# High weights against both halves of the activations in one 512-column product: the up-projections of a two-layer encoder

## The chip, the core and the metric

The kernel runs on one core of a Trainium2 chip. The metric is the device time of one execution in microseconds (us); of several runs the median is taken. PE is TensorE, PEld its weight load, DVE is VectorE, ACT is ScalarE, POOL is GpSimd, SP is SyncE, which issues the DMAs.

## What is computed

The reference is a trunk of two layers on 256 tokens of width 2048: a token mixer (attention), then a channel mixer, each with a normalization before and after and with shifts, scales and gates that come from a conditioning vector. The channel mixer is the part that the change touches, with `D_FF` = 5504:

```python
def conv_ffn(h, w_up, conv_w, conv_b, w_down):
    gate, up = jnp.split(h @ w_up, 2, axis=-1)
    gp = jnp.pad(gate, ((0, 0), (1, 1), (0, 0)))
    gate = gp[:, :-2] * conv_w[0] + gp[:, 1:-1] * conv_w[1] + gp[:, 2:] * conv_w[2] + conv_b
    return (jax.nn.gelu(gate, approximate=True) * up) @ w_down
```

All of it is in float32. The convolution runs over the tokens, with three taps per feature.

## The kernel before

**Products in three parts.** A float32 product is made of products of rounded halves: each operand is a high part (its rounding to the type `fp32r`) plus a low part (the rest). Of the four products of halves three are computed: high weights with high activations, high weights with low activations, low weights with high activations. The activations of the up-projection stand in the tile `hT`, laid out `[128, 16, 2, 256]`: 16 tiles of 128 input features (k), then high and low, then 256 tokens. So the high and low halves of one k-tile lie side by side, 512 columns in a row.

**The stream of weights.** All weights pass through one stream (class `Stream`, object `st`), in an order that a plan fixes. A unit of 512 KB (128 x 1024) lands in one of nine `raw` buffers. ScalarE copies it to its high part `whi` (line 259), VectorE subtracts to get the low part `wlo` (line 309, method `lows`). There are four buffers of each (`SPLIT_BUFS`), so a unit can be split once PE has finished the unit four before it. Between the weight units lie units of the modulation matrix `ada_w`, which VectorE multiplies and adds up itself (line 284).

**Ticks.** When PE's products of a unit have been written down, `st.done` is called: it frees the unit's buffers, lets the stream go on (which writes down the split of a further unit and any modulation steps), makes one tick of a clock of units, and then writes down the low parts. `st.chain` spreads the steps that follow an accumulator over the ticks after it, one step per tick, so that they stand between the splits on ScalarE and VectorE.

**The channel mixer** (`ffn`, line 1031) works on two parts of the 5504 features, 22 and 21 blocks of 128. In each part it takes two blocks at a time: 256 features of the gate, then the same 256 of the up side. One accumulator is one PSUM bank, seen as two blocks of 256 tokens (`packed`). `feat_units` (line 639) runs over the 16 k-tiles, four to a unit, and for each block makes three products of 256 columns, with the weights as the stationary operand: lines 655, 657 and 658. There are eight banks, handed out in turn.

After the gate's accumulator `gate` lets ScalarE write the middle tap with the bias to `cv`, at once; one tick later VectorE adds the two outer taps, reading the bank; one tick later ScalarE applies the gelu. After the up accumulator, `up` lets VectorE multiply `cv` with the bank (line 1058), one tick later ScalarE rounds it to the high half of `act`, and one tick later VectorE subtracts for the low half. When a part is done, `out_chunks` multiplies `act` with the down-projection's weights in products of 512 columns (lines 622 to 624).

In layer 0 the first seven accumulators (`PRE`) are built side by side before the rest, over k-tiles as they become ready. In layer 1 the first accumulator is begun while the normalization before it is still running (`f_head`), and finished in the loop.

Of the kernel before, what the change touches and what calls it, by code (L numbers as in the profile page):

```python
# [9 lines left out]
F32 = mybir.dt.float32  # L10
F32R = mybir.dt.float32r
I32 = mybir.dt.int32
AF = mybir.ActivationFunctionType
# [3 lines left out]
D, S, P = 2048, 256, 128  # L17
KT = D // P
DFF = 5504
NF = DFF // P  # L20
# [168 lines left out]
def encoder_kernel(ctx: ExitStack, tc: tile.TileContext, x, c, ada_w, ada_b, norm_g,  # L189
                   ab_w_in, ab_w_out, a_sink, c_w_in, c_w_out, c_lambda, c_subln_g,  # L190
                   ffn_w_up, ffn_conv_w, ffn_conv_b, ffn_w_down, out):
    nc = tc.nc
# [6 lines left out]
    def bank():  # L199
        return psum.tile([P, 512], F32, name="bank", bufs=8)  # L200
# [4 lines left out]
    def vy():  # L205
        return cp.tile([P, 2, D], F32, name="vy")
# [187 lines left out]
    st = Stream()  # L394
    mods, cur = {}, {}
# [81 lines left out]
    def sums():  # L477
        s = small("ssq", 5)
        nc.gpsimd.memset(s[:, 4:5], EPS)
        return s  # L480
# [8 lines left out]
    def square_sum(src, dst, n=D):  # L489
        j = tmp.tile([P, 512], F32, name="junk", bufs=1)  # L490
        nc.scalar.activation(j[:, :src.shape[1]], src, AF.Square, scale=n ** -0.5, accum_out=dst)  # L491
# [147 lines left out]
    def feat_units(acc, k0, kn, n):  # L639

        hT = cur["hT"]
        kt = k0
        while kt < k0 + kn:
            i, (hi, lo) = st.take()
            a = hi.shape[1]
            for b in range(a):
                k = kt + b
                for j in range(n // P):
                    wh = hi[:, b, j * P:(j + 1) * P]
                    if lo is None:  # L650
                        nc.tensor.matmul(acc[:, j], wh, cur["h"][:, k], start=k == 0 and j == 0, stop=k == KT - 1,
                                         skip_group_check=True)
                        continue
                    wl = lo[:, b, j * P:(j + 1) * P]
                    nc.tensor.matmul(acc[:, j], wh, hT[:, k, 0], start=k == 0 and j == 0, stop=False,  # L655
                                     skip_group_check=True)
                    nc.tensor.matmul(acc[:, j], wh, hT[:, k, 1], start=False, stop=False, skip_group_check=True)  # L657
                    nc.tensor.matmul(acc[:, j], wl, hT[:, k, 0], start=False, stop=k == KT - 1,  # L658
                                     skip_group_check=True)
            kt += a  # L660
            st.done(i)

    def packed():
        return bank().rearrange("p (j n) -> p j n", j=2)

# [6 lines left out]
    def feat_pair(pool, scale, name, bufs=1):  # L672
        acc = packed()
        feat_units(acc, 0, KT, 256)
        return feat_out(pool, acc, scale, name, bufs)
# [355 lines left out]
    def ffn(l, pool, next_norm, pre=0, head=None, first=()):  # L1031
        y = None
        ssq = [sums() for t in range(2)]
        cw = cwc[l]

        def gate(acc, cv, j, nj):
            def taps(_):
                for i in range(nj):
                    w0, w2 = cw[:, j + i:j + i + 1], cw[:, 2 * NF + j + i:2 * NF + j + i + 1]
                    nc.vector.scalar_tensor_tensor(cv[:, i, 1:], g[:, i, :S - 1], w0, cv[:, i, 1:],  # L1040
                                                   op0=ALU.mult, op1=ALU.add)
                    nc.vector.scalar_tensor_tensor(cv[:, i, :S - 1], g[:, i, 1:S], w2, cv[:, i, :S - 1],
                                                   op0=ALU.mult, op1=ALU.add)

            def gelu(_):
                nc.scalar.activation(cv[:, :nj], cv[:, :nj], AF.Gelu_apprx_tanh)

            g = acc
            for i in range(nj):
                w = cw[:, NF + j + i:NF + j + i + 1]  # L1050
                nc.scalar.activation(cv[:, i], g[:, i, :S], AF.Identity,
                                     bias=cw[:, 3 * NF + j + i:3 * NF + j + i + 1], scale=w)
            st.chain(taps, gelu)

        def up(acc, cv, act, j, nj):
            c = cv[:, :nj]
            ah = act[:, j:j + nj, 0]
            st.chain(lambda _: nc.vector.tensor_mul(c, acc[:, :nj], c),
                     lambda _: nc.scalar.activation(ah, c, AF.Copy),
                     lambda _: nc.vector.tensor_tensor(act[:, j:j + nj, 1], c, ah.bitcast(F32), op=ALU.subtract))  # L1060

        for part, (f0, fn) in enumerate(PARTS):
            act = pool.tile([P, 22, 2, S], F32R, name="act", bufs=1)
            p = pre if part == 0 else 0
            accs = [packed() for _ in range(p)]
            for n, (k0, k1) in enumerate(zip(FK, FK[1:])) if p else ():
                if n:
                    st.advance(plan.mid[n - 1])
                    st.flush()
                for k in range(k0, k1, 4):  # L1070
                    for t in range(2):
                        Affine(t, k, cur[t][:, k:k + 4], mods[0, 4], mods[0, 3], AFF1[t]).high().low()
                st.advance()
                for a in range(p):
                    feat_units(accs[a], k0, k1 - k0, 2 * P)
                    if k1 == KT:
                        if a % 2 == 0:
                            cv = pool.tile([P, 2, S], F32, name="cv", bufs=2)
                            gate(accs[a], cv, a, 2)
                        else:  # L1080
                            up(accs[a], cv, act, a - 1, 2)
            with tc.manual_schedule(engines=ORDERED) if pre else nullcontext():
                for j in range(p // 2 * 2, fn, 2):
                    nj = min(2, fn - j)
                    for k in range(2):
                        if j + k < p:
                            continue
                        if first:
                            acc = first.pop()
                            feat_units(acc, 4, KT - 4, nj * P)  # L1090
                        else:
                            acc = packed()
                            feat_units(acc, 0, KT, nj * P)
                        if k == 0:
                            cv = pool.tile([P, 2, S], F32, name="cv", bufs=2)
                            gate(acc, cv, f0 + j, nj)
                        else:
                            up(acc, cv, act, j, nj)
                final = part == len(PARTS) - 1
                y = y or vy()  # L1100

                def evac(acc, t, ch, then=None):
                    c0 = ch * 512
                    yc = y[:, t, c0:c0 + 512]
                    if part == 0:
                        nc.scalar.activation(yc, acc, AF.Copy)
                        return
                    z = tmp.tile([P, 512], F32, name="hf", bufs=3) if final else yc
                    nc.vector.tensor_add(z, acc, yc)
                    if final:  # L1110
                        square_sum(z, ssq[t][:, ch:ch + 1])
                        nc.vector.tensor_mul(yc, z, mods[l, 5][:, c0:c0 + 512])
                    if then:
                        then()

                out_chunks(act, list(range(fn)), evac, 0, 0,
                           (lambda: [next_norm(t, y, ssq[t]) for t in range(2)]) if final else None, head=head)
# [28 lines left out]
    with tc.tile_pool(name="at0", bufs=1, reuse_waits="tile") as pool:  # L1146
# [22 lines left out]
        for k in range(4):  # L1169
            b = bank()  # L1170
# [18 lines left out]
        for q, (k0, k1) in enumerate(zip(GK, GK[1:])):  # L1189
            st.advance(plan.mark[q])  # L1190
            st.flush()
            n = k1 - k0
# [4 lines left out]
            hT = cur["hT"]  # L1197
# [18 lines left out]
        for l in range(2):  # L1216
            cw = ffn_conv_w[l].rearrange("t (j p) -> (t j) p", p=P)
# [52 lines left out]
    with tc.tile_pool(name="at1", bufs=1, reuse_waits="tile") as pool:  # L1270
        v = vy()
        oT = pool.tile([P, KT, 2, S], F32R, name="oT")
        for ch in range(4):
            if ch == 0:
                acc = v_acc
# [4 lines left out]
            else:  # L1280
                acc = [bank(), bank()]
# [3 lines left out]
        for h in range(8):  # L1285
            k = feat_pair(pool, 1.0, "kc")
# [4 lines left out]
    with tc.tile_pool(name="ff1", bufs=1, reuse_waits="tile") as pool:  # L1291
        ffn(1, pool, lambda t, y, ssq: Norm(t, y, ssq), first=f_acc)
# [27 lines left out]
```

## Time and profile before

| | us |
|---|---|
| median of 3 runs | 2290.14 |
| lowest and highest | 2285.76, 2291.74 |
| the profiled execution | 2286.51 |
| its span | 2284.7 |
| PE, DVE, ACT busy | 2204.5, 1625.5, 1058.2 |

The span is the time from the first to the last instruction of the profiled execution; 1.8 us of its time lie around it. Busy time is the union of an engine's instructions. A product's duration runs from its start to its modelled end, and products are pipelined: a new one begins before the one ahead of it has ended, so durations do not add up to the span. TensorE's clock was granted in full for nearly all of the span (0.986 on the mean).

In the rows of the profile a group reads: line, engine, operation, written tile, read tiles, shapes, count, busy time, mean duration, then the idle time of the engine before it and what ended that. The up-projections of layer 0 run from about 370 to 628 us and from 755 to 997 us, those of layer 1 from about 1540 to 1795 us and from 1918 to 2158 us; the down-projections lie between and behind.

### The profile page before, as it was taken

What the parts mean: (1) busy time and instruction counts of PE and PEld (TensorE: products, weight loads), DVE (VectorE), ACT (ScalarE), POOL (GpSimd) and SP (SyncE); (2) the same over time, 40 slices, a digit from 0 to 9 for tenths busy, and PEclk for the clock granted to TensorE, in tenths of its full rate; (3) what the DMA queues carried; (4) which work ended last, traced back from release to release, by engine and by line L of the source; (5) the groups of instructions that cost most, each with busy time, mean ns of one, the idle gap of its engine ahead of it and who ended that gap; (6) DMA issues with size and microseconds to landing.
All of it is one profiled execution on the core that took longest, in us unless ns stands there. A gap on an engine that the chain in (4) does not pass through costs nothing.

```text
span 2284.7 us, 37384 instructions
## 1 busy us (share of the span) xinstructions
PE 2204.5 (96%) x14961; PEld 2022.2 (89%) x14961; DVE 1625.5 (71%) x1802; ACT 1058.2 (46%) x1451; POOL 44.4 (2%) x72
## 2 busy tenths in 40 slices
PE   5689999999999999999999999999999999999998
PEld 3679987999988999988789998879999888999986
DVE  7888987888866777876778986557656545565554
ACT  4344456544434444444644554455444434444443
POOL 0000000000000000000001100000000000000000
PEclk9889999999999999999999999999999999999999
DMA  9999998988888888987599996656666666666652
GB/s 338 365 330 325 327 316 283 315 294 291 285 291 303 283 289 286 299 288 249 169 347 323 303 304 206 220 172 188 208 196 204 200 204 205 195 203 203 178 188 102
DMA packets 390427, 587.14 MB, mean 257 GB/s; under 512 B 18110, under 2 KB 256360, under 8 KB 389612
## 3 DMA queue, kind: packets, MB, share of 16 engines
q1 hardware_dynamic: 390252, 584.75, 78.0%
q8 instruction: 117, 1.92, 0.3%
q14 instruction: 58, 0.48, 0.1%
HBM read 582.58 MB, written 2.10 MB: 256 GB/s over the span
## 4 chain that ended last, share of the span: by engine, by line
PE 82%; issue 12%; DVE 3%; DMA 1%; ACT 1%; POOL 1%; DVEq 0%; POOLq 0%; ACTq 0%
PE bank L655 17%; PE bank L657 17%; PE bank L658 17%; PE bank L622 9%; PE bank L623 9%; PE bank L624 9%; DVE aacc L284 2%; PE bank L459 1%; DMA raw<-in_ab_w_in_dram 1%; PE bank L794 1%; DVE wlo L309 1%; PE bank L523 1%; DMA raw<-in_ada_w_dram 0%; POOL rs_r L486 0%; ACT junk L491 0%
## 5 line engine op out<-in xcount | busy, mean ns | idle before, releaser
L259 ACT ACTIVATE whi<-raw 128x1024 fp32r<-128x1024 f32 x708 | 745.6, 1055 | 980.8 <-PE bank L657 493.0
L309 DVE TENSOR_TENSOR wlo<-raw,whi 128x1024 fp32r<-128x1024 f32 x708 | 860.6, 1219 | 474.5 <-ACT whi L259 466.0
L655 PE MATMUL bank<-hT,whi 128*128 128x256 f32 x3616 | 1026.4, 284 | 0.0
L658 PE MATMUL bank<-hT,wlo 128*128 128x256 f32 x3616 | 1017.1, 281 | 5.9 <-DVE wlo L309 5.9
L657 PE MATMUL bank<-hT,whi 128*128 128x256 f32 x3616 | 1016.4, 281 | 0.2 <-DVE hT L518 0.2
L658 PEld LDWEIGHTS bank<-hT,wlo 128*128 128x128 f32 x3616 | 683.8, 189 | 7.7 <-DVE wlo L309 7.7
L655 PEld LDWEIGHTS bank<-hT,whi 128*128 128x128 f32 x3616 | 684.1, 189 | 3.1 <-ACT whi L259 1.2
L657 PEld LDWEIGHTS bank<-hT,whi 128*128 128x128 f32 x3616 | 684.0, 189 | 3.2 <-issue 1.7
L284 DVE SCALAR_TENSOR_TENSOR aacc<-raw,ccol,aacc 128x1024 f32<-128x1024 f32 x352 | 453.8, 1289 | 53.9 <-DMA raw<-in_ada_w_dram 51.9
L622 PE MATMUL bank<-whi,act 128*128 128x512 f32 x656 | 259.3, 395 | 0.0
L623 PE MATMUL bank<-wlo,act 128*128 128x512 f32 x656 | 258.9, 395 | 0.0
L624 PE MATMUL bank<-whi,act 128*128 128x512 f32 x656 | 258.9, 395 | 0.0
L624 PEld LDWEIGHTS bank<-whi,act 128*128 128x128 f32 x656 | 123.4, 188 | 29.3
L623 PEld LDWEIGHTS bank<-wlo,act 128*128 128x128 f32 x656 | 123.5, 188 | 28.9
L622 PEld LDWEIGHTS bank<-whi,act 128*128 128x128 f32 x656 | 123.4, 188 | 28.9
L622 PE MATMUL bank<-whi,hT 128*128 128x512 f32 (+1 forms) x192 | 75.4, 398 | 14.6 <-ACT hT L514 14.6
L623 PE MATMUL bank<-wlo,hT 128*128 128x512 f32 (+1 forms) x192 | 74.6, 391 | 0.0
L624 PE MATMUL bank<-whi,hT 128*128 128x512 f32 (+1 forms) x192 | 71.7, 383 | 0.0
L622 PE MATMUL bank<-whi,oT 128*128 128x512 f32 x176 | 71.1, 404 | 0.0
L623 PE MATMUL bank<-wlo,oT 128*128 128x512 f32 x176 | 69.6, 396 | 0.0
L624 PE MATMUL bank<-whi,oT 128*128 128x512 f32 x176 | 69.5, 395 | 0.0
L486 POOL TENSOR_TENSOR rs_r<-rs_m,mhalf 128x1 f32<-128x1 f32 x32 | 23.8, 752 | 1901.5 <-DVE rs_m L484 1901.5
(168 smaller groups left out, 1378.1 us busy)
## 6 DMA issues: line engine op xcount, KB each, us to landing
raw<-in_ada_w_dram SPq DMA_DIRECT2D x384, 512.0 KB, 5.5
raw<-in_ffn_w_up_dram SPq DMA_DIRECT2D x344, 512.0 KB, 4.7
raw<-in_ffn_w_down_dram SPq DMA_DIRECT2D x168, 512.0 KB, 5.0
raw<-in_c_w_in_dram SPq DMA_DIRECT2D x96, 512.0 KB, 5.2
raw<-in_ab_w_in_dram SPq DMA_DIRECT2D x56, 512.0 KB, 6.4
raw<-in_c_w_out_dram SPq DMA_DIRECT2D x32, 512.0 KB, 5.2
raw<-in_ab_w_out_dram SPq DMA_DIRECT2D x16, 512.0 KB, 5.6
gb<-in_norm_g_dram SPq DMA_DIRECT2D x3, 1024.0 KB, 4.9
```

What stands on the lines that cost most here:

```text
L259: nc.scalar.activation(hi, v, AF.Copy)
L284: nc.vector.scalar_tensor_tensor(self.acc, t, col, self.acc, op0=ALU.mult, op1=ALU.add)
L309: nc.vector.tensor_tensor(lo, v, hi.bitcast(F32), op=ALU.subtract)
L459: nc.tensor.matmul(t[:, j:j + 1], acc[:, j * P:(j + 1) * P], ones[:, 0:1], start=True, stop=rows is None)
L486: nc.gpsimd.tensor_tensor(r, m, mhalf, op=ALU.pow)
L523: nc.tensor.transpose(ps[:, q * P:(q + 1) * P], src[:, q * P:(q + 1) * P], ident)
L622: nc.tensor.matmul(dst, ah, hi, start=first, stop=False, skip_group_check=True)
L623: nc.tensor.matmul(dst, ah, lo, start=False, stop=False, skip_group_check=True)
L624: nc.tensor.matmul(dst, al, hi, start=False, stop=last, skip_group_check=True)
L655: nc.tensor.matmul(acc[:, j], wh, hT[:, k, 0], start=k == 0 and j == 0, stop=False, skip_group_check=True)
L657: nc.tensor.matmul(acc[:, j], wh, hT[:, k, 1], start=False, stop=False, skip_group_check=True)
L658: nc.tensor.matmul(acc[:, j], wl, hT[:, k, 0], start=False, stop=k == KT - 1, skip_group_check=True)
```

## The change

A second routine, `feat_wide`, takes the place of `feat_units` for the accumulators of the loop in `ffn`, except for the seven early ones of layer 0 and the one of layer 1 that was begun early. It gives each block of 128 features a bank of its own. The high weights meet `hT[:, k]`, high and low halves together, in one product of 512 columns; the low weights meet the high half, 256 columns, and add to the first half of the bank. So the bank ends up with two sums side by side, and a function `both` adds them: ScalarE copies the second half to a tile `gsum` in SBUF, VectorE adds the first half to it. What followed then reads `gsum` in place of the bank, and starts one tick later.

```diff
+    def feat_wide(n):
+        hT = cur["hT"]
+        accs = [packed() for _ in range(n // P)]
+        kt = 0
+        while kt < KT:
+            i, (hi, lo) = st.take()
+            a = hi.shape[1]
+            for b in range(a):
+                k = kt + b
+                for j, acc in enumerate(accs):
+                    nc.tensor.matmul(acc, hi[:, b, j * P:(j + 1) * P], hT[:, k], start=k == 0, stop=False,
+                                     skip_group_check=True)
+                    nc.tensor.matmul(acc[:, 0], lo[:, b, j * P:(j + 1) * P], hT[:, k, 0], start=False,
+                                     stop=k == KT - 1, skip_group_check=True)
+            kt += a
+            st.done(i)
+        return accs
...
-            g = acc
-            for i in range(nj):
-                w = cw[:, NF + j + i:NF + j + i + 1]
-                nc.scalar.activation(cv[:, i], g[:, i, :S], AF.Identity,
-                                     bias=cw[:, 3 * NF + j + i:3 * NF + j + i + 1], scale=w)
-            st.chain(taps, gelu)
+            if isinstance(acc, list):
+                st.chain(lambda _: both(acc), conv, taps, gelu)
+            else:
+                conv(acc)
+                st.chain(lambda _: taps(acc), gelu)
+
+        def both(accs):
+            g = pool.tile([P, 2, S], F32, name="gsum", bufs=2)
+            for i, a in enumerate(accs):
+                nc.scalar.activation(g[:, i], a[:, 1], AF.Copy)
+                nc.vector.tensor_add(g[:, i], a[:, 0], g[:, i])
+            return g
...
-            st.chain(lambda _: nc.vector.tensor_mul(c, acc[:, :nj], c),
+            wide = isinstance(acc, list)
+            st.chain(*([lambda _: both(acc)] if wide else []),
+                     lambda g: nc.vector.tensor_mul(c, (g if wide else acc)[:, :nj], c),
...
-                            acc = packed()
-                            feat_units(acc, 0, KT, nj * P)
+                            acc = feat_wide(nj * P)
```

`conv` holds the lines that `gate` had before, unchanged.

On PE, at the first accumulator of the loop in layer 0 (bank 4358, right behind the last of the seven early ones, bank 3340), there stood before:

```order
L658 MATMUL bank_3340<-hT_3162,wlo_4195 128x256
L655 MATMUL bank_4358<-hT_3162,whi_4229 128x256
L657 MATMUL bank_4358<-hT_3162,whi_4229 128x256
L658 MATMUL bank_4358<-hT_3162,wlo_4230 128x256
L655 MATMUL bank_4358<-hT_3162,whi_4229 128x256
L657 MATMUL bank_4358<-hT_3162,whi_4229 128x256
L658 MATMUL bank_4358<-hT_3162,wlo_4230 128x256
```

and now, where the second block has bank 4359:

```order
L658 MATMUL bank_3340<-hT_3162,wlo_4195 128x256
L674 MATMUL bank_4358<-hT_3162,whi_4229 128x512
L676 MATMUL bank_4358<-hT_3162,wlo_4230 128x256
L674 MATMUL bank_4359<-hT_3162,whi_4229 128x512
L676 MATMUL bank_4359<-hT_3162,wlo_4230 128x256
```

Each three products have become two; the products ahead of this place stand as they did.

On DVE, behind the first gate accumulator of that loop (its sum is `gsum_4592`), with the low half of a unit (`wlo`), a modulation step (`aacc`) and the last step of an early accumulator (`act`) around it, there stood before:

```order
L1060 TENSOR_TENSOR act_3333<-cv_4353,act_3333 128x2x256
L284 SCALAR_TENSOR_TENSOR aacc_4078<-raw_4456,ccol_67,aacc_4078 128x1024
L309 TENSOR_TENSOR wlo_4617<-raw_4425,whi_4616 128x1024
L1040 SCALAR_TENSOR_TENSOR cv_4625<-bank_4492,cwc0_71,cv_4625 128x255
L1042 SCALAR_TENSOR_TENSOR cv_4625<-bank_4492,cwc0_71,cv_4625 128x255
L1040 SCALAR_TENSOR_TENSOR cv_4625<-bank_4492,cwc0_71,cv_4625 128x255
L1042 SCALAR_TENSOR_TENSOR cv_4625<-bank_4492,cwc0_71,cv_4625 128x255
```

and now:

```order
L1095 TENSOR_TENSOR act_3333<-cv_4353,act_3333 128x2x256
L1085 TENSOR_TENSOR gsum_4592<-bank_4461,gsum_4592 128x256
L1085 TENSOR_TENSOR gsum_4592<-bank_4462,gsum_4592 128x256
L309 TENSOR_TENSOR wlo_4588<-raw_4437,whi_4587 128x1024
L284 SCALAR_TENSOR_TENSOR aacc_4078<-raw_4482,ccol_67,aacc_4078 128x1024
L309 TENSOR_TENSOR wlo_4615<-raw_4458,whi_4614 128x1024
L1066 SCALAR_TENSOR_TENSOR cv_4568<-gsum_4592,cwc0_71,cv_4568 128x255
L1068 SCALAR_TENSOR_TENSOR cv_4568<-gsum_4592,cwc0_71,cv_4568 128x255
```

The two additions stand ahead of a unit's low half, and the taps, which read the bank before, come two units later and read `gsum`.

On ACT, at the same place, there stands now:

```order
L259 ACTIVATE whi_4587<-raw_4437 128x1024
L1084 ACTIVATE gsum_4592<-bank_4461 128x256
L1084 ACTIVATE gsum_4592<-bank_4462 128x256
L259 ACTIVATE whi_4614<-raw_4458 128x1024
L1059 ACTIVATE cv_4568<-gsum_4592,cwc0_71 128x256 x2
```

The two copies that the additions wait for stand behind the split of a unit, `whi_4587`, whose low half waits on DVE behind those additions.

More of the change, by code (lines that the diff above doesn't have):

```diff
@@ L1036, in gate, with conv, taps @@
         def gate(acc, cv, j, nj):
-            def taps(_):
+            def conv(g):
+                for i in range(nj):
+                    w = cw[:, NF + j + i:NF + j + i + 1]
+                    nc.scalar.activation(cv[:, i], g[:, i, :S], AF.Identity,
+                                         bias=cw[:, 3 * NF + j + i:3 * NF + j + i + 1], scale=w)
+                return g
+            def taps(g):
                 for i in range(nj):
@@ L1046, in gelu @@
                 nc.scalar.activation(cv[:, :nj], cv[:, :nj], AF.Gelu_apprx_tanh)
-            g = acc
-            for i in range(nj):
-                w = cw[:, NF + j + i:NF + j + i + 1]
-                nc.scalar.activation(cv[:, i], g[:, i, :S], AF.Identity,
-                                     bias=cw[:, 3 * NF + j + i:3 * NF + j + i + 1], scale=w)
-            st.chain(taps, gelu)
+            if isinstance(acc, list):
[8 more added lines that the diff above has]
+                nc.vector.tensor_add(g[:, i], a[:, 0], g[:, i])
+            return g
         def up(acc, cv, act, j, nj):
```

## The prediction

> **What bounds the kernel now.** I read the page first (busy times, the chain that ended last, the costliest groups), then the busy time by stretches, then PE's instructions in order of time at the seams between wide and narrow products, then VectorE's and ScalarE's at the place that worries me most.
>
> ```profile
> PE 2204.5 (96%) x14961; PEld 2022.2 (89%) x14961; DVE 1625.5 (71%) x1802; ACT 1058.2 (46%) x1451; POOL 44.4 (2%) x72
> ...
> PE 82%; issue 12%; DVE 3%; DMA 1%; ACT 1%; POOL 1%; DVEq 0%; POOLq 0%; ACTq 0%
> ...
> L259 ACT ACTIVATE whi<-raw 128x1024 fp32r<-128x1024 f32 x708 | 745.6, 1055 | 980.8 <-PE bank L657 493.0
> L309 DVE TENSOR_TENSOR wlo<-raw,whi 128x1024 fp32r<-128x1024 f32 x708 | 860.6, 1219 | 474.5 <-ACT whi L259 466.0
> L655 PE MATMUL bank<-hT,whi 128*128 128x256 f32 x3616 | 1026.4, 284 | 0.0
> L658 PE MATMUL bank<-hT,wlo 128*128 128x256 f32 x3616 | 1017.1, 281 | 5.9 <-DVE wlo L309 5.9
> ...
> L622 PE MATMUL bank<-whi,act 128*128 128x512 f32 x656 | 259.3, 395 | 0.0
> ```
>
> TensorE is the bound: busy 96% of the span, 82% of the chain, and the products of the projections cost it no idle time but 5.9 us before line 658. The others wait for it: ScalarE's split of the weights (line 259) stood 493 us behind products of line 657, VectorE's low half (line 309) 466 us behind that split. The tempting reading is wrong, though: 281 ns for 256 columns against 395 ns for 512 looks as if one wide product replaced two narrow ones at a gain of 167 ns. The durations overlap: 3616 products of 281 ns on each of three lines make 3,060 us, more than the span. What counts is the step from one product to the next. I get it from stretches that hold only one kind, as (stretch + one duration) / count, since the count takes in products that lie partly inside.
>
> ```profile
> 760.00:820.00 60.00, 60.00 (x508) 1.00 0.91 295
> 910.00:990.00 80.00, 80.00 (x684) 1.00 0.91 297
> 1570.00:1790.00 220.00, 220.00 (x1877) 1.00 0.66 201
> 1930.00:2090.00 160.00, 160.00 (x1351) 1.00 0.67 202
> 1010.00:1090.00 80.00, 80.00 (x346) 1.00 0.78 255
> 1800.00:1900.00 100.00, 100.00 (x430) 1.00 0.64 203
> 2170.00:2270.00 100.00, 100.00 (x432) 1.00 0.46 147
> ```
>
> The columns are the stretch, its length, PE's busy time with its count, the granted clock (1.00 throughout), DMA share and GB/s. The first four hold 256-column products of the up-projections: 60.28/508 = 118.7 ns, 80.28/684 = 117.4, 220.28/1877 = 117.4, 160.28/1351 = 118.6. There are two steady steps, 117.4 and 118.6, in both layers, and no idle time. The last three hold 512-column products of the down-projections: 80.395/346 = 232.4, 100.395/430 = 233.5, 100.395/432 = 232.4 ns. So two narrow products take 234.7 to 237.3 ns and one wide one 232.4 to 233.5: time goes almost wholly by columns, and the columns do not change.
>
> **The products, the only term with weight.** Both layers have 86 blocks of 128 features; in layer 0 seven accumulators of two blocks keep the old form, in layer 1 the one begun early, so 72 + 84 = 156 blocks with 16 k-tiles each, 2,496 triples. A triple is now 3 x 117.4 = 352.1 to 3 x 118.6 = 355.9 ns, middle 354.0. Afterwards it is one wide and one narrow product: 232.4 + 117.4 = 349.8 to 233.5 + 118.6 = 352.1, middle 350.9. That holds if alternating costs nothing. The kernel has single seams of both kinds, here where layer 0 goes from up- to down-projection and back:
>
> ```profile
> 628.59 0.28 PE L658 MATMUL bank<-hT,wlo 128*128 128x256 f32 x1
> 628.71 0.39 PE L622 MATMUL bank<-whi,act 128*128 128x512 f32 x1
> 628.94 0.39 PE L623 MATMUL bank<-wlo,act 128*128 128x512 f32 x1
> ...
> 754.90 0.40 PE L624 MATMUL bank<-whi,act 128*128 128x512 f32 x1
> 755.13 0.29 PE L655 MATMUL bank<-hT,whi 128*128 128x256 f32 x1
> 755.26 0.28 PE L657 MATMUL bank<-hT,whi 128*128 128x256 f32 x1
> ```
>
> Narrow to wide takes 0.12 us, the wide one after it 0.23; wide to narrow 0.23, the narrow one after it 0.13. So a seam shows no charge, but for the last step, which may be some 10 ns over. I take 350.9: 354.0 - 350.9 = 3.1 ns, times 2,496 = 7.7 us gained. The ends are a slow pairing after a fast step (352.1 - 352.1 = 0) and a fast pairing after a slow step (355.9 - 349.8 = 6.1 ns, 15.2 us).
>
> The Trainium skill, "TensorE: Matmul & The Clock Gate", section "Back-to-back issue gap", gives N/2.4 + 2.5 ns for an isolated product of N columns, so that merging two saves one fixed 2.5 ns; by it the term would be an estimated 6.2 us. The trace agrees in the small fixed part (2 x 117.4 - 232.4 = 2.4 ns, 2 x 118.6 - 233.5 = 3.7), not in the rate: 512 columns take 232.4 ns and not the rule's 216.
>
> **What leaving PSUM costs.** Each block gains one ScalarE copy and one VectorE addition of 128x256. Nearest rows, with the stretches that show what room both engines have (columns: PE, PEld, DVE, ACT, POOL, clock, DMA):
>
> ```profile
> L680 DVE TENSOR_TENSOR oT<-bank,oT 128x256 fp32r<-128x256 f32 x8 | 3.3, 419 | 0.2 <-ACT oT L679 0.2
> ...
> L679 ACT ACTIVATE oT<-bank 128x256 fp32r<-128x256 f32 x8 | 2.9, 367 | 1.2 <-PE bank L701 1.2
> ...
> 770.00:960.00 190.00, 190.00 (x1611) 190.00 (x1610) 149.73 (x160) 86.17 (x99) 0.00 (x0) 1.00 0.89 291
> ...
> 1560.00:1780.00 220.00, 220.00 (x1877) 220.00 (x1877) 134.06 (x148) 104.60 (x120) 0.00 (x0) 1.00 0.66 202
> ```
>
> 156 x 0.42 = 65.5 us on VectorE and 156 x 0.37 = 57 us on ScalarE, in a span where PE is the bound. An accumulator of two blocks takes PE 96 products x 118 ns = 11.3 us, four units of 2.83 us. VectorE is busy 149.73/190 = 79% in layer 0 and 134.06/220 = 61% in layer 1; 0.84 us more per 11.3 us makes 86% and 68%. ScalarE goes from 45% to about 52%. So this work lies under the products. The convolution, the two taps and the product with the gate read SBUF instead of PSUM afterwards; each is one instruction as before, and I put nothing down for it.
>
> The change also adds a wait: VectorE's addition stands until ScalarE's copy is done, ScalarE's copy stands behind the split of the next unit, and behind the additions stand VectorE's low half of that unit (which PE needs) and a modulation step. How late may a low half be? There are four split buffers, so a unit is split when PE has finished the fourth before it, and PE comes to it 3 x 2.83 = 8.5 us later.
>
> ```profile
> 780.90 1.06 ACT L259 ACTIVATE whi<-raw 128x1024 fp32r<-128x1024 f32 x1 [1.84 <-PE bank L657]
> ...
> 781.99 1.23 DVE L309 TENSOR_TENSOR wlo<-raw,whi 128x1024 fp32r<-128x1024 f32 x1 [0.48 <-ACT whi L259]
> ...
> 458.16 1.07 ACT L259 ACTIVATE whi<-raw 128x1024 fp32r<-128x1024 f32 x1 [1.27 <-PE bank L657]
> ...
> 462.84 1.22 DVE L309 TENSOR_TENSOR wlo<-raw,whi 128x1024 fp32r<-128x1024 f32 x1
> ```
>
> Usually the low half is done 781.99 + 1.23 - 780.90 = 2.3 us after the split begins. With copy, addition, second addition ahead of it that is 2.3 + 0.37 + 2 x 0.42 = 3.5 us, inside 8.5. The worst I found is 464.06 - 458.16 = 5.9 us, where the seven early accumulators of layer 0 are drained together; those keep the old form. I charge 0 us; without that cover every late microsecond would be PE's, as the 5.9 us of line 658 are.
>
> An accumulator takes two of the eight banks instead of one. They are handed out in turn, so the fifth accumulator reuses the first's, which is read one unit (2.83 us) after its end, while PE is 3 x 11.3 us from needing it: 0 us. DMA brings the same bytes, at 0.89 of its share in layer 0, in a stretch about 1% shorter: 0 us.
>
> **Sum.** The profiled execution took 2286.51 us, a span of 2284.7 and 1.8 around it; with 7.7 us off it would take 2278.8. The median of the three runs is 2290.14, 3.6 above it, so I forecast 2290.14 - 7.7 = 2282.4 us.
>
> **Rivals.**
> *Alternating disturbs the steady step (slower).* At each change from wide to narrow PE would lose time that a run of equal products does not. Against it: the seams above. For it: that one 0.13, up to 12 ns over the step, and that no stretch alternates for long. From 3.1 ns per pair the sign turns, from 5.9 ns it is slower by over 0.3%. At 10 ns: (10 - 3.1) x 2,496 = 17 us, 2307.
> *VectorE falls behind in layer 0.* It needs 8.9 + 0.84 us per 11.3; were a full split and copy (1.06 + 0.37) spent idle each time as well, 11.2 of 11.3 would be gone. Half a microsecond over, for layer 0's 36 accumulators, is 18 us of PE, a net 10 us slower, 2300; half of such cases end near 2290. Against it: that idle time lies where VectorE now waits for the split anyway.
> *The weight load sets the narrow step.* If so, the narrow product, with a wide one to hide a load behind, would fall to its own time. The shortest reload step in the trace is at one-column products:
>
> ```profile
> 899.46 1.70 PE L459 MATMUL bank<-ones,aacc 128*128 128x1 f32 x14
> ```
>
> (1.70 - 0.27)/13 = 110 ns, close under 117.4. A triple would then be at best 232.4 + 110 = 342.4: 11.6 x 2,496 = 29 us, 2261. Against it: 512 columns have twice the time for one load and are no faster per column. The Trainium skill (same page, section "LDWEIGHTS") puts a load of 128 columns at 128/1.2 = 107 ns; by that the load nearly fills the narrow step, and this rival is what would follow if it did.
> *The steady step falls badly.* Two steps exist and I do not know what picks one; 352 to 354 ns per pair leaves 0 to 5 us, about 2288.
> That the change does not do what it says is ruled out by the order: the triples are pairs, nothing before them moves.
>
> **Chances.** 0.3% is 6.9 us, about what a measurement of this kernel can tell from no change. Forecast 67% (by the spread of 0 to 15.2 us around 7.7: 42 over the bound, 25 within); bad step 12%, within; alternating charged 9%, slower; VectorE behind 6%, half within, half slower; load-bound 6%, faster. Faster 0.48, same 0.40, slower 0.12. The range leaves out the charge (2307), half of VectorE's case and the full load gain (2261): 2270 to 2294.
>
> **What would show it.** In the profile after: 2,496 products of 512 and as many of 256 columns in the up-projections; pairs per stretch at 350 to 352 ns; VectorE some 65 us and ScalarE some 57 us busier; PE's idle time before the low product still a few us. A step of the pair above 354, or a long idle time of PE behind the low half in layer 0, would prove me wrong; so would a pair under 347.

## The result and the profile after

The changed kernel takes 2269.6 us (median of 4 runs, 2267.57 to 2272.47) against 2289.93 before: ratio 0.9914, 95% interval 0.9901 to 0.9926, so 20.3 us faster. The direction was forecast; the gain was forecast at 7.7 us, and the median lies 0.4 us under the low end of the range.

From the page of the changed kernel, the busy times, the chain, and the groups that answer to those shown of before:

```profile
PE 2193.5 (97%) x12465; PEld 1907.1 (84%) x12465; DVE 1679.9 (74%) x1958; ACT 1105.4 (49%) x1607; POOL 44.1 (2%) x72
...
PE 82%; issue 12%; DVE 3%; ACT 1%; DMA 1%; POOL 1%; DVEq 0%; POOLq 0%; ACTq 0%
...
L674 PE MATMUL bank<-hT,whi 128*128 128x512 f32 x2496 | 867.2, 392 | 0.0
L676 PE MATMUL bank<-hT,wlo 128*128 128x256 f32 x2496 | 697.5, 280 | 0.0
...
L658 PE MATMUL bank<-hT,wlo 128*128 128x256 f32 x1120 | 318.1, 284 | 5.6 <-DVE wlo L309 5.6
...
L1085 DVE TENSOR_TENSOR gsum<-bank,gsum 128x256 f32<-128x256 f32 x156 | 62.1, 419 | 35.6 <-ACT gsum L1084 35.6
L1084 ACT ACTIVATE gsum<-bank 128x256 f32<-128x256 f32 x156 | 54.8, 374 | 59.8 <-PE bank L676 59.8
```

The counts are as worked out: 2,496 wide and 2,496 narrow products, with no idle time before either, and 156 copies and additions at 374 and 419 ns (0.37 and 0.42 were taken). PE is still the bound, with the same 82% of the chain. VectorE's additions stood 35.6 us behind the copies, as the new wait said they would, and the products show no idle time for it. Over the span VectorE is 54.4 us busier (1679.9 - 1625.5) and ScalarE 47.2 (1105.4 - 1058.2), some 10 us less each than forecast.

The stretches of one kind of product (length, PE busy with its count, clock, DMA share, GB/s), of the changed kernel in layer 1:

```profile
1600.00:1760.00 160.00, 160.00 (x925) 1.00 0.70 207
1950.00:2100.00 150.00, 150.00 (x867) 1.00 0.70 207
```

The mean duration of a wide and a narrow product is 0.336 us, so 160.336/925 = 173.3 and 150.336/867 = 173.4 ns per product, 346.7 per pair. The forecast was 350.9, with 349.8 to 352.1 as bounds. Against the 354.0 of the old triple the pair saves 7.3 ns, times 2,496 = 18.2 us: that is the whole of the gain within its interval (17 to 23 us). From start to start in the same trace (1600 to 1760 us, mean) a narrow product takes 117.5 ns, as before, and a wide one 229.2, where the down-projections of the prediction have 232.4 to 233.5. So it is the wide product whose step came out short.

The two profiled executions differ by only 14.0 us (2286.51 and 2272.47, the latter the slowest of its four). The other 4 us or so of the 18.2 lie outside the change, in the attention stage of layer 1, where TensorE's clock was granted less often in this execution: before, then after,

```profile
1385.00:1420.00 35.00, 31.93 (x250) 1.00 0.63 201
1420.00:1560.00 140.00, 135.27 (x719) 0.98 0.61 193
```

```profile
1377.00:1412.00 35.00, 33.13 (x229) 0.90 0.62 198
1412.00:1552.00 140.00, 135.75 (x699) 0.96 0.58 188
```

The third figure from the right of each row is the granted clock: 0.90 against 1.00, then 0.96 against 0.98. So the medians, not the two profiled executions, tell the gain.

### The profile page after: what moved, and what is told of

Same layout as the page of the kernel before. It is cut to its first block, busy times and chain, and to the rows that moved or that the text cites. A ratio compares the mean times of both kernels' runs of the same rounds, so it can differ in the third digit from the quotient of the medians.

```text
span 2270.7 us, 32680 instructions
## 1 busy us (share of the span) xinstructions
PE 2193.5 (97%) x12465; PEld 1907.1 (84%) x12465; DVE 1679.9 (74%) x1958; ACT 1105.4 (49%) x1607; POOL 44.1 (2%) x72
## 4 chain that ended last, share of the span: by engine, by line
PE 82%; issue 12%; DVE 3%; ACT 1%; DMA 1%; POOL 1%; DVEq 0%; POOLq 0%; ACTq 0%
PE bank L674 25%; PE bank L676 13%; PE bank L622 10%; PE bank L624 10%; PE bank L623 9%; PE bank L655 4%; PE bank L657 4%; PE bank L658 4%; DVE aacc L284 2%; PE bank L459 1%; PE bank L813 1%; DMA raw<-in_ab_w_in_dram 1%; PE bank L523 1%; DVE wlo L309 0%; POOL rs_r L486 0%
## 5 line engine op out<-in xcount | busy, mean ns | idle before, releaser
L674 PE MATMUL bank<-hT,whi 128*128 128x512 f32 x2496 | 867.2, 392 | 0.0
L674 PEld LDWEIGHTS bank<-hT,whi 128*128 128x128 f32 x2496 | 468.6, 188 | 103.9 <-ACT whi L259 0.7
L655 PE MATMUL bank<-hT,whi 128*128 128x256 f32 x1120 | 326.6, 292 | 0.0
L657 PE MATMUL bank<-hT,whi 128*128 128x256 f32 x1120 | 317.6, 284 | 0.2 <-DVE hT L518 0.2
L655 PEld LDWEIGHTS bank<-hT,whi 128*128 128x128 f32 x1120 | 215.1, 192 | 2.5 <-issue 0.5
L657 PEld LDWEIGHTS bank<-hT,whi 128*128 128x128 f32 x1120 | 214.8, 192 | 2.7 <-issue 1.0
L622 PE MATMUL bank<-whi,hT 128*128 128x512 f32 (+1 forms) x192 | 76.4, 403 | 14.6 <-ACT hT L514 14.6
L1085 DVE TENSOR_TENSOR gsum<-bank,gsum 128x256 f32<-128x256 f32 x156 | 62.1, 419 | 35.6 <-ACT gsum L1084 35.6
L1084 ACT ACTIVATE gsum<-bank 128x256 f32<-128x256 f32 x156 | 54.8, 374 | 59.8 <-PE bank L676 59.8
```

What stands on the lines that cost most here:

```text
L622: nc.tensor.matmul(dst, ah, hi, start=first, stop=False, skip_group_check=True)
L674: nc.tensor.matmul(acc, hi[:, b, j * P:(j + 1) * P], hT[:, k], start=k == 0, stop=False, skip_group_check=True)
L1085: nc.vector.tensor_add(g[:, i], a[:, 0], g[:, i])
```

## The experiments

Three theories were set against each other for the term that had come out too small. **A**: a wide and a narrow product in strict turn run in less time than either among its like. **B**: wide products are faster when they stream the activations. **C**: each product that is saved saves a fixed charge. All edits are made to the changed kernel.

**The merged product undone, the rest kept** (x1_narrow).

```diff
-                    nc.tensor.matmul(acc, hi[...], hT[:, k], ...)
+                    for s in range(2):
+                        nc.tensor.matmul(acc[:, s], hi[...], hT[:, k, s], ...)
```

> The merged product undone, all else of the change kept (two banks, copy and addition, later chain): high weights meet the high and the low half in two products of 256 columns. If the whole gain is in the products, the three take 352 to 356 ns again instead of 346.7, 5.3 to 9.3 ns x 2,496 = 13 to 23 us more than the changed kernel, so 2283 to 2293 us, no change from before within about 4 us. If instead the separate banks or the later evacuation brought the gain, it stays at about 2270.

Measured: 2290.76 us, before 2288.58, ratio 1.0007 (0.9998 to 1.0017): the whole gain is gone.

```profile
1600.00:1760.00 160.00, 160.00 (x1350) 1.00 0.65 201
```

160.281/1350 = 118.7 ns per product, 356 per triple, as before. So the gain is in the products; banks, copies, additions and the later chain bring or cost nothing that shows beside an interval of some 4 us.

**The same products, grouped** (x2_grouped): wide, wide, narrow, narrow.

```diff
                 for j, acc in enumerate(accs):
                     nc.tensor.matmul(acc, hi[...], hT[:, k], ...)
+                for j, acc in enumerate(accs):
                     nc.tensor.matmul(acc[:, 0], lo[...], hT[:, k, 0], ...)
```

> The same products in another order: per k-tile two wide ones (one for each block), then two narrow ones, instead of wide, narrow, wide, narrow. Theory A (a wide product is short, 229.2 ns, because it stands between narrow ones): a wide one behind a wide one takes 232.4 to 233.5, so two pairs take 696.5 to 698 ns instead of 693.3, 1.6 to 2.3 ns more per pair, 4 to 6 us, 2274 to 2276. Theory B (a wide product that streams the activations takes 229.2 wherever it stands) and theory C (each product removed saves a fixed 7.4 ns): 346.7 per pair, 2270 within 2.

Measured: 2278.58 us, ratio 0.9955 (0.9940 to 0.9970), half of the gain.

```profile
1600.00:1760.00 160.00, 160.00 (x912) 1.00 0.66 204
```

160.336/912 = 175.8, 351.6 ns per pair, 4.9 more than in strict turn, where A expected 348.3 to 349. From start to start in this trace (same stretch) a wide product before a wide one takes 232.9 ns, a wide one before a narrow one 234.6, a narrow one before a narrow one 118.3, before a wide one 117.5. So A is not merely off in size: here each wide product has a narrow one beside it, and neither of the two is short. What is left of A is the strict turn, a wide product with narrow ones on both sides. B and C both ask for 346.7 here, since products and operands are the same and as many; neither can be the whole. And 351.6 lies inside the bounds that the prediction had put together from pure stretches (349.8 to 352.1).

**Only wide products** (x3_lowwide): the low weights meet both halves too, which adds low with low.

```diff
-                    nc.tensor.matmul(acc[:, 0], lo[...], hT[:, k, 0], ...)
+                    nc.tensor.matmul(acc, lo[...], hT[:, k], ...)
```

> The low weights too meet both halves of the activations in one product of 512 columns (a fourth partial product, low with low, is added): only wide products, all streaming the activations. Theory A: each takes 232.4 to 233.5 ns as in the down-projection, a pair 465 to 467, 118 to 120 ns x 2,496 = 295 to 300 us more than the changed kernel, 2565 to 2570. Theory B: each takes 229.2, a pair 458.4, 279 us more, 2549. Theory C gives no figure for it.

Measured: 2570.15 us (one run), at the upper end of A's figure.

```profile
1750.00:1950.00 200.00, 200.00 (x855) 1.00 0.50 153
```

200.395/855 = 234.4 ns: a wide product that streams the activations is no faster than one of the down-projection (232.4 to 233.5). B falls.

**The way out of PSUM done twice** (x4_twice): `both` runs its copy and addition two times for each block.

> The copy and the addition out of PSUM done twice for every block, in place, the second copy waiting for the first addition: 57 us more on ScalarE, 65 us more on VectorE. If this work lies wholly under the products, as the prediction says, the time stays at 2270 within 3 us and PE has no idle time before the up-projections' products. If VectorE is near its edge in layer 0 (86% would become 93%, with longer waits between), PE waits there for low halves: 5 to 30 us more.

Measured: 2266.0 us, ratio 0.9895 (0.9878 to 0.9911), whose interval overlaps the change's own. In layer 0 VectorE's share rose further (first the changed kernel, then this one; PE, PEld, DVE, ACT), and PE went through as many products:

```profile
770.00:960.00 190.00, 190.00 (x1109) 167.70 (x1108) 163.63 (x195) 98.56 (x136) 0.00 (x0) 1.00 0.89 295
```

```profile
770.00:960.00 190.00, 190.00 (x1109) 167.56 (x1108) 173.82 (x228) 109.67 (x169) 0.00 (x0) 1.00 0.90 296
```

163.63/190 = 86% became 91%, at no cost that shows. The cover was larger than it needed to be.

**Strict turn across blocks, and from another place** (y2_cross, y6_half). In the first each narrow product belongs to the other block (`m` is the number of blocks), so that the bank changes inside a pair. In the second the narrow product streams the low half of the activations (low with low is computed, low weights with high activations left out).

```diff
-                    nc.tensor.matmul(acc[:, 0], lo[:, b, j * P:(j + 1) * P], hT[:, k, 0], ...)
+                    o = m - 1 - j
+                    nc.tensor.matmul(accs[o][:, 0], lo[:, b, o * P:(o + 1) * P], hT[:, k, 0], ...)
```

```diff
-                    nc.tensor.matmul(acc[:, 0], lo[...], hT[:, k, 0], ...)
+                    nc.tensor.matmul(acc[:, 0], lo[...], hT[:, k, 1], ...)
```

> Strict turn of wide and narrow kept, but each narrow product belongs to the other block: wide for block 0, narrow for block 1, wide for block 1, narrow for block 0. So the bank changes at every second product inside a pair instead of between pairs. If the strict turn is what makes the pair short, it stays at 346.7 ns and the time at 2266 to 2272. If it is that the narrow product follows the wide one into the same bank (which the grouped order gave up too), the pair goes to about 351.6 as in the grouped order, 12 us more, 2276 to 2282.

> The narrow product streams the low half of the activations instead of the high half (so it computes low with low, and low weights with high activations are left out): the same order and banks, another place of the 256 columns. If the place from which the narrow product reads matters, the pair's 346.7 ns changes, to 350 or 352 as in the other orders (8 to 13 us more); if only order counts, it stays and the time is 2266 to 2272.

Measured: 2272.36 and 2270.28 us (one run each). The stretch of y2_cross, then of y6_half:

```profile
1600.00:1760.00 160.00, 160.00 (x925) 1.00 0.67 207
```

```profile
1600.00:1760.00 160.00, 160.00 (x925) 1.00 0.67 206
```

925 products again in both, 346.7 ns per pair. So it matters neither whether the narrow product follows the wide one into the same bank nor from which half it reads. How often the bank changes is not settled: it changes at every second product in the changed kernel and in y2_cross, but at every product in the grouped order. It changes at every second product in x3_lowwide too, at 234.4 ns, so that pace alone does not make a wide product short; but the grouped order gave up both the strict turn and that pace, and no run parts the two.

**Three narrow products in another order** (y7_order): high with high, low with high, high with low.

> Three narrow products again, in the order high with high, low with high, high with low. If three narrow products cost 352 to 356 ns in any order, the time is that of the kernel before, 2284 to 2293. If a change of the weights between any two products is what matters (here all three follow other weights), the triple moves out of 352 to 356 by more than 2 ns and the time by 5 us or more.

Measured: 2292.85 us (one run), before 2290.1 beside it.

```profile
1600.00:1760.00 160.00, 160.00 (x1351) 1.00 0.65 200
```

160.281/1351 = 118.6, 355.9 per triple, as in the old order. Elsewhere narrow products have a third step, which the up-projections of the kernel before do not show, in x1_narrow and then in this run:

```profile
440.00:500.00 60.00, 60.00 (x502) 1.00 0.92 311
525.00:575.00 50.00, 50.00 (x419) 1.00 0.91 296
```

60.283/502 = 120.1 and 50.283/419 = 120.0 ns.

**How short can the narrow product get** (x5_n128)? Here it has 128 columns; the low weights' share for the other 128 tokens is left out.

```diff
-                    nc.tensor.matmul(acc[:, 0], lo[...], hT[:, k, 0], ...)
+                    nc.tensor.matmul(acc[:, 0, :P], lo[...], hT[:, k, 0, :P], ...)
```

> The low weights meet the high activations of the first 128 tokens only (this leaves out the low weights' share for the other 128). If the load of weights bounds a short product, the narrow step falls from 117.5 only to about 110 to 112 ns, as at one-column products, and the pair to 339 to 341: 14 to 19 us less than the changed kernel, 2250 to 2256. If only columns count, it falls to about 59 ns, the pair to 288, 146 us less, about 2125, and VectorE would become the bound in layer 0.

Measured: 2251.87 us (one run), inside the load's figure.

```profile
1600.00:1760.00 160.00, 160.00 (x943) 1.00 0.67 206
```

The mean duration is 0.332 us, so 160.332/943 = 170.0 and a pair takes 340.0 ns. Half of the narrow product's columns, some 58 ns, are gone, and 6.7 are saved. The rows of the products, then of the loads, show where the rest went:

```profile
1699.87 0.22 PE L676 MATMUL bank<-hT,wlo 128*128 128x128 f32 x1
1699.92 0.44 PE L674 MATMUL bank<-hT,whi 128*128 128x512 f32 x1
1700.21 0.22 PE L676 MATMUL bank<-hT,wlo 128*128 128x128 f32 x1
```

```profile
1699.87 0.19 PEld L674 LDWEIGHTS bank<-hT,whi 128*128 128x128 f32 x1
1699.98 0.19 PEld L676 LDWEIGHTS bank<-hT,wlo 128*128 128x128 f32 x1
1700.21 0.19 PEld L674 LDWEIGHTS bank<-hT,whi 128*128 128x128 f32 x1
```

The narrow product did become short: the wide one starts 0.05 us after it. But the wide one now takes 0.29 from start to start (means over the stretch: 58 and 282 ns, against 117.5 and 229.2 in the changed kernel). The load of low weights follows the load of high weights after 0.11 us and not after 0.06, and the next load of high weights comes 0.23 later; the two make up the pair's 0.34. 0.11 is the step of the one-column products (110 ns), each with a load of its own. I read from this that the load now sets the pair, and that the wide product pays for it; beyond the forecast that came true, no run tests this.

**A narrow product of 384 columns** (x8_n384), adding low with low for half of the tokens.

> The low weights meet 384 columns instead of 256 (adding low with low for half of the tokens). By columns alone the second product takes 384 x 0.458 = 176 ns; theory A in its plain form (short wide product beside a shorter one) keeps the wide one at 229.2, so a pair of about 405 ns, 58 ns x 2,496 = 146 us more than the changed kernel, 2416. If the short turn needs the exact 2 to 1 of columns, the wide one goes back to 232.4 to 234.4 and the pair to 409 to 411: 155 to 160 us more, 2425 to 2430.

Measured: 2419.99 us (one run), between the two figures.

```profile
1650.00:1850.00 200.00, 200.00 (x985) 1.00 0.57 175
```

With a mean duration of 0.365 us: 200.365/985 = 203.4, 406.8 ns per pair, where A's plain form says 405 and pure stretches 409 to 411. From start to start the wide product takes 230.9 ns here: the strict turn still helps at 512 to 384, though less.

**Carried to the other projections** (x6_attn): the 24 accumulators of the attention stages made with `feat_wide`, ScalarE's copy and a VectorE addition behind each.

> On top of the change, the projections of the attention stages too (24 accumulators of two blocks, 768 triples) are made of wide and narrow products in turn. If the pair's 346.7 ns is a matter of the order of products alone, 768 x (352 to 356 - 346.7) = 4 to 7 us less than the changed kernel: 2262 to 2266 if that is at 2269. If the attention chains, which use up to eight banks in short turns, wait for banks or for the extra addition, the gain is lost there or more: 2268 to 2280.

Measured: 2274.62 us, ratio 0.9926 (0.9909 to 0.9943): not shown to be faster or slower than the change alone (0.9901 to 0.9926). PE's waits in the attention stage of layer 1, in the changed kernel and in this one (time, count, longest):

```profile
PE bank L813 <- ACT qc L688: 4.3, 3, 2.2
```

```profile
PE bank L816 <- DVE qc L696: 9.6, 8, 1.9
```

The score products come right behind the projection and now wait for the addition, once in each of eight heads. There the way out of PSUM lies on the path, and 5.3 us more of waiting meet the 512 x 7.3 = 3.7 us that this stage's products could save. In these two traces, though, that stage takes as long in both, within 1 us; the loss lies in layer 0, whose up-projections begin at 371.1 and 373.9 us. Its attention stage, in the changed kernel and in this one:

```profile
155.00:300.00 145.00, 145.00 (x1108) 1.00 0.95 321
155.00:300.00 145.00, 141.80 (x834) 0.99 0.93 315
```

PE has no idle time there in the first and 3.2 us in the second, 2.6 of them before a wide product that, by the profile, waits for a bank which VectorE has still to read:

```profile
PE bank L674 <- DVE smb L778: 2.6, 1, 2.6
```

**Carried to the 512-column triples** (x7_tok): the middle one of three wide products cut in two, so that wide and narrow alternate.

```diff
         nc.tensor.matmul(dst, ah, hi, ...)
+        if n == 512:
+            nc.tensor.matmul(dst[:, :256], ah, lo[:, :256], ...)
+            nc.tensor.matmul(dst, al, hi, ...)
+            nc.tensor.matmul(dst[:, 256:], ah, lo[:, 256:], ...)
+            return
```

> On top of the change, every triple of 512-column products of the down-projections, the output projections and the values (1024 of them) becomes wide, narrow, wide, narrow: the middle one is cut into two of 256 columns. Theory A (wide and narrow in strict turn are short whatever they stream): 2 x 346.7 = 693.4 ns instead of 697 to 700, 3.9 to 6.6 ns x 1024 = 4 to 7 us less than the changed kernel, 2262 to 2266. Theory C (each product carries a fixed charge): one product more per triple, 2.4 to 7 ns x 1024 = 2 to 7 us more, 2271 to 2277. If the short turn belongs to streaming the activations alone: no gain, 2269 to 2272.

Measured: 2276.95 us, ratio 0.9934 (0.9917 to 0.9952).

```profile
1800.00:1900.00 100.00, 100.00 (x572) 1.00 0.60 204
```

With a mean duration of 0.339 us: 100.339/572 = 175.4, four products take 701.7 ns where three wide ones take 697 to 700. No gain, rather 2 to 5 ns lost. From start to start the wide product takes 230.6 ns here and the narrow one 120.6, against 229.2 and 117.5. So theory A as it stood does not hold for every strict turn. Here the stationary operand is the activations and the streamed one the weights; I could not tell which difference decides.

## Why the direction was right and the size was not

*The steady steps.* Right: reading the overlapping durations as steps would have promised 167 ns per triple, the steps promised a few, and a few it was.

*The pair.* This is the term that was mis-sized. The step "afterwards it is one wide and one narrow product: 232.4 + 117.4 = 349.8 to 233.5 + 118.6 = 352.1" took each product's step from a stretch of its like and held that alternating costs nothing. It costs less than nothing: 346.7 ns, below both ends, because the wide product takes 229.2 and not 232.4 to 233.5. The grouped order, which sets two of a kind side by side, gives 351.6, so the sum holds for that order and not for the one written. By the steps, of the 7.3 ns per triple some 2.4 come with the merging (354.0 to 351.6) and 4.9 with the order. By the times the merging has a larger part: the grouped kernel is 10.0 us faster than the kernel before (2288.58 - 2278.58, interval 7 to 14), about half of the 20.3; 2.4 x 2,496 = 6.0 us would be a third of the 18.2. So the direction was earned by what the prediction named, the merging; half or more of the gain came from an order effect that it put at nothing, and that the median ends within 0.4 us of the range is in that part luck. The seam rows could not show this: they are single steps to a hundredth of a microsecond, and the difference is 3 ns in 232.

The prediction also said that a pair under 347 would prove it wrong. The pair is at 346.7: by its own test this step of it failed.

By the rule of the Trainium skill, "TensorE: Matmul & The Clock Gate", section "Back-to-back issue gap", the saving would have been 2.5 ns per triple, an estimated 6.2 us. The traces agree with it in size for the merging alone (2.4 ns from the middle of the old step, 0.5 to 4.3 from its two ends, 352.1 and 355.9). No sequence is in that rule, and here the sequence is worth as much again by the times and twice as much by the steps.

*The way out of PSUM.* Right where it counts: 86% of VectorE in layer 0 and 0 us on the path; even twice the work cost nothing that shows. The sums were a little high (65.5 and 57 us were worked out, and the rows of the additions and copies have 62.1 and 54.8), for the reason that the prediction itself gives for products: durations overlap. The two additions in the row below last 0.76 us together and not 2 x 0.42. The new wait was priced at a low half 3.5 us after its split begins, against 8.5 us that PE leaves; in the changed kernel behind such a pair of additions:

```profile
788.30 1.06 ACT L259 ACTIVATE whi<-raw 128x1024 fp32r<-128x1024 f32 x1 [1.71 <-PE bank L674]
```

```profile
789.66 0.76 DVE L1085 TENSOR_TENSOR gsum<-bank,gsum 128x256 f32<-128x256 f32 x2 [1.22 <-ACT gsum L1084]
790.33 1.22 DVE L309 TENSOR_TENSOR wlo<-raw,whi 128x1024 fp32r<-128x1024 f32 x1
```

790.33 + 1.22 - 788.30 = 3.25 us.

*The rivals.* Alternating was charged a price in the slower rival; it earned one. VectorE did not fall behind. The load does not set the narrow step at 256 columns, which stayed at 117.5 ns; at 128 columns the loads follow each other at 0.11 and 0.23 us, and the pair is as long as both. The bad step did not come: strict turn of 512 and 256 columns in the up-projections has one steady step in every run shown, where narrow products among themselves go at 117.4, 118.6 or, in two runs, 120.0.

Left open is why strict turn has a shorter step, and why it does not at the down-projection. The runs rule out, as the whole cause, that the narrow product shares the wide one's bank, the place of the streamed columns, and the number of products. How often the bank changes is not parted from the order.

## What to carry to other kernels

Where the tensor engine is the bound, a merged product saves the fixed part of a step and not half of it: read steps from counts in pure stretches, never from overlapping durations. Then time the very sequence that the kernel will run, since the order of the same products moved the step by 1.4% here (346.7 against 351.6), which was half of the gain by the times and two thirds by the steps. Extra work behind the products is free while they cover it, and is not where a product waits for its result, as in the attention heads.

## What the runs showed of the hardware that I had not expected

- Wide and narrow products in strict turn take 346.7 ns per pair (512 + 256 columns), grouped in twos 351.6, and three narrow ones 352 to 360, at a granted clock of 1.00. In strict turn the wide product is the shorter one: 229.2 ns from start to start, against 232.4 to 234.6 with another wide one beside it.
- The same turn with the activations as the stationary operand takes 350.8 ns per pair (2 x 175.4).
- A pair of 512 + 128 columns takes 340.0 ns: the narrow product has 58 ns from start to start, the wide one 282, and their loads start 0.11 and 0.23 us apart.
- Narrow products among themselves have steady steps of 117.4, 118.6 and, in x1_narrow and y7_order, 120.0 ns, which hold for tens of us and differ from run to run. What picks one stays open.
